# Issue order in a two-layer decoder kernel: the sums and the cast of the next weight tile ahead of the deferred work, its residues behind it

## The chip, the cores and the metric

One NeuronCore of one Trainium2 chip runs the whole program. The metric is the device time of one execution in microseconds, as the median over runs. Engines are named as in the profile: PE (TensorE, matrix products; PEld is its loading of weights), DVE (VectorE), ACT (ScalarE), POOL (GpSimd) and SP (SyncE, which issues the loads of weights).

## What is computed

A decoder trunk of two layers on 256 tokens of width 2048, in float32. Layer 0 mixes by dilated sliding-window attention, layer 1 by multi-head latent attention. Behind each mixer stands a SwiGLU of hidden width 5632, and the change touches only how these two SwiGLUs (the FFNs) are issued. Cut to what matters here:

```python
D_MODEL, SEQ, DEPTH, FFN_HIDDEN = 2048, 256, 2, 5632

def swiglu(xn, w_gu, w_down):
    g, u = jnp.split(xn @ w_gu, 2, axis=-1)
    return (jax.nn.silu(g) * u) @ w_down

for layer in range(DEPTH):
    ...                                        # layer 0: dilated attention, layer 1: latent attention
    h = h + swiglu(rms_norm(h, ffn_norm_g[layer]), ffn_w_gu[layer], ffn_w_down[layer])
return rms_norm(h, final_norm_g)
```

## The kernel before

**Products in three terms.** A float32 operand is split into a high part `hi` (a cast to the type fp32r, by ACT) and a residue `lo = raw - hi` (a subtraction on DVE). A product is then three matmuls, hi by hi, hi by lo and lo by hi, accumulated in PSUM; in `mul` these are L694, L695 and L696. Activations are kept split and transposed (`xT`, `hT`: the high halves, then the low halves).

**The stream of weights.** `WeightStream` holds all weight tiles of the program in the order in which they are used. `load` issues the DMA of a tile (1 MB, on SP's queue) into one of three `raw` slots; `split` makes `hi` and `lo` of it, in three slots each (`ahead + 1`). `next()` is called once per tile: it advances, splits up to two tiles beyond the current one, loads up to three beyond the last one split, and returns the parts of the current tile. So while the products of tile k are issued, the tile two further on is the last that has been split.

**Seven products for eight.** In the FFN the tiles come as pairs of 128-row blocks by two times 512 columns. In an "eight" pair the four blocks are multiplied with two token halves in 24 matmuls. In a "seven" pair (`kp` 2, 4 and 6 of the eight pairs of a block, except in the first block of a layer) sums of blocks replace one of the eight products: 21 matmuls. Its weight tile needs three additions on DVE beforehand (L182 to L184), and the sums get parts of their own, `th` (ACT) and `tl` (DVE). The operand's side needs sums as well (`sums`, L662 to L669, which writes `forms` or `forms_h`).

**Blocks.** `ffn` runs three parts of 16, 16 and 12 column tiles. In a part, each `j` (4 tiles) is one call of `mixed` for gate and up, eight pairs; then two calls for the down projection (`c` = 0 and 2, parts 0 and 1 alone); part 2's down projection goes through `product`. `mixed` accumulates the left half (`la`, gate) and the right half (`ra`, up) and calls `close(0, la)` in the middle of the last pair and `close(1, ra)` at its end. `close(0, ...)` returns the SiLU (L756) as a function that is issued behind the split of a tile (`ws.more()`), and `close(1, ...)` multiplies (L760).

**Deferred work.** `Later` holds functions that become due some tiles later; `later.tick()`, once per pair, issues those that are due. In the FFN these are:
- `turned`, due behind pair 0 of the next block: transposes `up` by PE (L406), splits it into `hT` (ACT L381, DVE L382), and calls `sums` for the pairs of the down projection that are "seven" (j = 4, 8 and 12 of parts 0 and 1);
- in the first block of a layer, behind pair 0, the last chunk of `transposed` with a gain (ACT L384, DVE L385) and `across` (DVE L435, PE L438, DVE L439), which lays a scale `R` out along the rows;
- `scaled(kp)`, behind pairs 2 to 7 of the first block and pairs 0 and 1 of the second: multiplies `xT` by `R` in place (L675), and calls `sums` for "seven" pairs.

**Who sets the order.** Inside the FFN, DVE and ACT run in the order in which the program issues (`tc.manual_schedule(engines=ORDERED)`). PE, POOL and SP are ordered by the framework's planner, which estimates when each instruction could start.

Of the kernel before, what the change touches and what calls it, by code (L numbers as in the profile page):

```python
# [10 lines left out]
F32 = mybir.dt.float32  # L11
F32R = mybir.dt.float32r
I32 = mybir.dt.int32
AF = mybir.ActivationFunctionType
ALU = mybir.AluOpType
AX = mybir.AxisListType

P = 128
# [70 lines left out]
class WeightStream:  # L89
# [4 lines left out]
    def __init__(self, nc, raw_pool, hl_pool, units, raw_bufs, ahead):  # L94
        self.nc, self.raw_pool, self.hl_pool, self.units = nc, raw_pool, hl_pool, units
        self.raw_bufs, self.ahead = raw_bufs, ahead
        self.raws, self.parts, self.sum_pool = {}, {}, None
        self.n_raw = self.n_split = self.at = 0

    def load(self, upto):  # L100
        while self.n_raw < min(upto, len(self.units)):
# [34 lines left out]
                    dst = [t.rearrange("p (o c) -> p o c", o=2) for t in dst]  # L136
                yield src, dst[0], dst[1], gain[:, k:k + 1]

    def split(self, upto):
        nc = self.nc  # L140
        while self.n_split < min(upto, len(self.units)):
            self.load(self.n_split + 1)
            raw = self.raws.pop(self.n_split)
            _, gain, form = self.units[self.n_split]
            if form in ("eight", "seven"):
                self.parts[self.n_split] = self.split_blocks(raw, form)
                self.n_split += 1
                continue
            _, nk, ncol = raw.shape
            if form == "dup":  # L150
                ncol *= 2
            hi = self.hl_pool.tile([P, 2048], F32R, tag="hi", name="hi", bufs=self.ahead + 1)
            lo = self.hl_pool.tile([P, 2048], F32R, tag="lo", name="lo", bufs=self.ahead + 1)
            view = lambda t: t[:, :nk * ncol].rearrange("p (k c) -> p k c", c=ncol)
            hi, lo = view(hi), view(lo)
            for src, h, l, g in self.pieces(raw, hi, lo, form, gain):
                if g is None:
                    nc.scalar.copy(out=h, in_=src)  # L158
                    nc.vector.tensor_tensor(out=l, in0=src, in1=h.bitcast(F32), op=ALU.subtract)  # L159
                else:  # L160
                    nc.scalar.activation(out=h, in_=src, func=AF.Copy, scale=g)
                    nc.vector.scalar_tensor_tensor(out=l, in0=src, scalar=g, in1=h.bitcast(F32),
                                                   op0=ALU.mult, op1=ALU.subtract)
            self.parts[self.n_split] = (hi, lo)
            self.n_split += 1

    def halve(self, hi, lo, src):
        self.nc.scalar.copy(out=hi, in_=src)  # L168
        self.nc.vector.tensor_tensor(out=lo, in0=src, in1=hi.bitcast(F32), op=ALU.subtract)  # L169

    def split_blocks(self, raw, form):

        hi, lo = [self.hl_pool.tile([P, 2048], F32R, tag=n, name=n, bufs=self.ahead + 1) for n in ("hi", "lo")]
        if form == "eight":
            self.halve(hi, lo, raw)
            return hi, lo
        th, tl = [self.sum_pool.tile([P, 1536], F32R, tag=n, name=n, bufs=1) for n in ("th", "tl")]
        sums = self.sum_pool.tile([P, 1536], F32, tag="sums", name="sums", bufs=1)  # L180
        v, w = [t.rearrange("p (i c) -> p i c", c=512) for t in (raw, sums)]
        self.nc.vector.tensor_tensor(out=v[:, 0], in0=v[:, 0], in1=v[:, 1], op=ALU.add)  # L182
        self.nc.vector.tensor_tensor(out=w[:, 1], in0=v[:, 0], in1=v[:, 2], op=ALU.subtract)
        self.nc.vector.tensor_tensor(out=w[:, 0::2], in0=v[:, 1::2],  # L184
                                     in1=w[:, 1].unsqueeze(1).broadcast_to([P, 2, 512]), op=ALU.subtract)
        self.halve(hi, lo, raw)
        self.halve(th, tl, sums)
        return hi, lo, th, tl

    def remaining(self):  # L190
        return len(self.units) - self.at
# [34 lines left out]
def kernel(ctx, tc, consts, x, attn_norm_g, ffn_norm_g, a_w_qkv, a_w_o, kv_norm_g,  # L226
                       b_w_kv_a, b_kv_a_norm_g, b_w_kv_b, b_w_q_a, b_q_a_norm_g, b_w_q_b, b_w_o,
                       ffn_w_gu, ffn_w_down, final_norm_g, out):
    nc = tc.nc
# [46 lines left out]
    rest = [ffn_norm_g.rearrange("l d -> (l d)"), kv_norm_g, b_kv_a_norm_g, b_q_a_norm_g[0]]  # L276
# [31 lines left out]
    for quad in range(HEADS // 4):  # L308
        for g in range(NG):
            k = 0  # L310
# [46 lines left out]
    later = Later()  # L357
# [283 lines left out]
    def ffn(xT, rstd, finish):  # L641

        with tc.tile_pool(name="ffn", bufs=1) as fp, tc.manual_schedule(engines=ORDERED):
# [35 lines left out]
            def mixed(X, pairs, seven, sums_of, left, right, close):  # L679

                la, ra = acc_tile(), acc_tile()
                pb, begun = None, set()

                def first(m):
                    new = m not in begun
                    begun.add(m)
                    return new  # L690

                def mul(out, x, w, i, st, sp):
                    (xh, xl), (wh, wl) = x, [t[:, i * 512:(i + 1) * 512] for t in w]
                    mm(out=out, lhsT=xh, rhs=wh, start=st, stop=False)  # L694
                    mm(out=out, lhsT=xh, rhs=wl, start=False, stop=False)  # L695
                    mm(out=out, lhsT=xl, rhs=wh, start=False, stop=sp)  # L696

                for kp in range(pairs):
                    ends = kp == pairs - 1
                    w = ws.next(late=ends)  # L700
                    x = lambda t, kk: [X[:, 2 * kp + kk, o + t * P:o + (t + 1) * P] for o in (0, S)]
                    if kp in seven:
                        i = seven.index(kp)
                        st, sp = i == 0, i == len(seven) - 1
                        if st:
                            pb = [bank() for _ in range(4)]
                        y = lambda j: x(1, 0) if j == 0 else [sums_of[:, i, h, j - 1, :] for h in range(2)]
                        mul(pb[0], x(0, 0), w[:2], 1, st, sp)
                        mul(la[:, 0], x(0, 1), w[:2], 3, first("la0"), False)
                        mul(pb[1], y(0), w[:2], 0, st, sp)  # L710
                        mul(ra[:, 0], y(3), w[:2], 2, first("ra0"), False)
                        mul(pb[3], y(2), w[2:], 0, st, sp)
                        mul(pb[2], y(1), w[2:], 1, st, sp)
                        mul(la[:, 1], x(1, 1), w[2:], 2, first("la1"), False)
                    else:
                        for i, (acc, m) in enumerate(((la, "la"), (ra, "ra"))):
                            for t in range(NT):
                                mul(acc[:, t], x(t, 0), w, 1 - i, first(f"{m}{t}"), False)
                                mul(acc[:, t], x(t, 1), w, 3 - i, False, ends)
                            if ends and i == 0:  # L720
                                then = close(0, la)
                                ws.more()
                                if then:
                                    then()
                    later.tick()
                    if seven and kp == seven[-1]:
                        nc.scalar.copy(out=left[:, 0], in_=pb[0])
                        nc.vector.tensor_tensor(out=left[:, 1], in0=pb[2], in1=left[:, 0], op=ALU.add)
                        nc.vector.tensor_tensor(out=left[:, 2], in0=pb[3], in1=left[:, 1], op=ALU.add)
                        nc.vector.tensor_tensor(out=right, in0=pb[1].unsqueeze(1).broadcast_to([P, NT, 512]),  # L730
                                                in1=left[:, 1:3], op=ALU.subtract)
                close(1, ra)

            def pair_tiles():
                return [fp.tile([P, n, 512], F32, tag=m, name=m) for m, n in (("gate", NT + 1), ("up", NT))]
# [1 line left out]
            for part, (k0, n) in enumerate(FFN_PARTS):  # L737
                last = part == len(FFN_PARTS) - 1
                hT = big_tile([P, 16, 2 * S], F32R, "hT")
                for j in range(0, n, 4):  # L740
# [7 lines left out]
                    def close(i, acc, first=first, both=(gate[:, 0:3:2], up), sc_=sc_):  # L748
                        d = both[i]
                        if not first:  # L750
                            nc.vector.tensor_tensor(out=d, in0=acc, in1=d, op=ALU.add)
                            acc = d

                        def silu():
                            for t in range(NT):
                                nc.scalar.activation(out=d[:, t], in_=acc[:, t], func=AF.Silu, scale=sc_[:, t:t + 1])  # L756
                        if i == 0:
                            return silu
                        for t in range(NT):
                            nc.vector.scalar_tensor_tensor(out=d[:, t], in0=acc[:, t], scalar=sc_[:, t:t + 1],  # L760
                                                           in1=both[0][:, t], op0=ALU.mult, op1=ALU.mult)
# [21 lines left out]
                def add(acc, c, t):  # L783
                    nc.vector.tensor_tensor(out=chunk(t, c), in0=acc[:, t, :], in1=chunk(t, c), op=ALU.add)
                    finish(c, t)
# [206 lines left out]
```

## Time and profile before

| what | value |
|---|---|
| median of 3 runs | 2678.03 us (2677.78 to 2679.45) |
| the profiled execution | 2679.72 us |
| its span, first to last instruction | 2677.9 us |
| PE busy | 2652.6 us, 99% of the span |
| PE loading weights | 2225.2 us, 83% |
| DVE busy | 2039.7 us, 76% |
| ACT busy | 1289.5 us, 48% |
| mean granted clock of PE | 0.998 |

A row of a timeline reads: start, duration, engine, line, operation, output <- inputs, shapes, count, and in brackets the engine's idle time just before it with what ended that. A row with a count over 1 stands for instructions in direct succession. Matmuls are pipelined: each is drawn longer than the distance to the next. The residue `lo` and the cast `hi` of FFN tiles are L169 and L168; `th`/`tl` have the same lines.

### The profile page before, as it was taken

The page shows a single profiled execution, that of the slowest core. Times are in us where ns is not written, and L with a number is a line of the kernel's source. Part 1 is how long each engine was busy: PE and PEld are TensorE (multiplying, and loading weights), DVE is VectorE, ACT ScalarE, POOL GpSimd, SP SyncE. Part 2 cuts the span into 40 slices and gives each one's busy share as a digit, 9 for nine tenths or more (in the row PEclk, how much of TensorE's full clock was granted, in tenths as well). Part 3 has the DMA queues.
Part 4 walks back from the last instruction along what each step waited for, and adds up shares of the span by engine and source line. Part 5 has one row for each costly group of instructions (what it writes and reads, how often), then busy time and mean ns, then how long its engine had stood idle before and what let it go on. Part 6 is the DMA issues. An engine that isn't in the chain of part 4 may idle for free. (4 is left out here: it accounts for less than half of the span.)

```text
span 2677.9 us, 32417 instructions
## 1 busy us (share of the span) xinstructions
PE 2652.6 (99%) x12914; PEld 2225.2 (83%) x12914; DVE 2039.7 (76%) x2458; ACT 1289.5 (48%) x1425; POOL 24.9 (1%) x28
## 2 busy tenths in 40 slices
PE   9999999999999999999999999999999999999998
PEld 7888888888888887788888888888887888888887
DVE  5676577477477659998899896588569988998985
ACT  5444444434444444554554454565445554544553
POOL 0000000000000000000000000000000000000000
PEclk9999999999999999999999999999999999999999
DMA  7545545555555555567567666544555676657663
GB/s 261 191 160 170 192 159 172 189 173 170 173 180 168 192 187 179 182 209 231 189 195 217 217 197 203 161 140 147 175 173 177 200 220 208 203 174 234 215 210 138
DMA packets 308088, 504.17 MB, mean 188 GB/s; under 512 B 13960, under 2 KB 117088, under 8 KB 307552
## 3 DMA queue, kind: packets, MB, share of 16 engines
q1 hardware_dynamic: 302960, 492.64, 55.8%
q0 software_dynamic: 4352, 8.39, 2.0%
q8 instruction: 101, 1.65, 0.2%
q10 hardware_dynamic: 624, 1.07, 0.1%
q14 instruction: 51, 0.42, 0.0%
HBM read 491.57 MB, written 2.10 MB: 184 GB/s over the span
## 5 line engine op out<-in xcount | busy, mean ns | idle before, releaser
L159 DVE TENSOR_TENSOR lo<-raw,hi 128x1024 fp32r<-128x1024 f32 (+2 forms) x450 | 514.7, 1167 | 338.9 <-ACT hi L158 322.7
L158 ACT CAST hi<-raw 128x1024 fp32r<-128x1024 f32 (+2 forms) x450 | 431.5, 1007 | 515.6 <-PE acc L451 291.1
L168 ACT CAST hi<-raw 128x2048 fp32r<-128x2048 f32 x240 | 458.7, 1912 | 430.9 <-issue 219.4
L169 DVE TENSOR_TENSOR lo<-raw,hi 128x2048 fp32r<-128x2048 f32 x240 | 549.4, 2290 | 76.5 <-ACT hi L168 67.8
L695 PE MATMUL acc<-lo,xT_f 128*128 128x512 f32 x988 | 387.4, 392 | 5.5 <-DVE lo L169 5.5
L694 PE MATMUL acc<-hi,xT_f 128*128 128x512 f32 x988 | 385.5, 392 | 2.7 <-ACT gate L756 2.7
L696 PE MATMUL acc<-hi,xT_f 128*128 128x512 f32 x988 | 385.4, 390 | 0.0
L451 PE MATMUL acc<-xT_a,hi 128*128 128x512 f32 x1536 | 379.4, 396 | 0.0
L451 PEld LDWEIGHTS acc<-xT_a,hi 128*128 128x128 f32 x1536 | 281.8, 189 | 53.5
L695 PEld LDWEIGHTS acc<-lo,xT_f 128*128 128x128 f32 x988 | 185.6, 188 | 48.1 <-DVE lo L169 9.9
L694 PEld LDWEIGHTS acc<-hi,xT_f 128*128 128x128 f32 x988 | 185.6, 188 | 42.9 <-ACT gate L756 3.6
L696 PEld LDWEIGHTS acc<-hi,xT_f 128*128 128x128 f32 x988 | 185.6, 188 | 39.0
L454 PEld LDWEIGHTS acc<-xT_a,lo 128*128 128x128 f32 x1536 | 196.9, 191 | 7.7
L454 PE MATMUL acc<-xT_a,lo 128*128 128x256 f32 x1536 | 199.3, 283 | 0.0
L169 DVE TENSOR_TENSOR tl<-sums,th 128x1536 fp32r<-128x1536 f32 x84 | 147.3, 1754 | 28.8 <-ACT th L168 28.8
L471 PE MATMUL acc<-lo,xT_a 128*128 128x512 f32 x384 | 150.4, 392 | 0.8 <-DVE lo L159 0.8
L472 PE MATMUL acc<-hi,xT_a 128*128 128x512 f32 x384 | 151.2, 394 | 0.0
L470 PE MATMUL acc<-hi,xT_a 128*128 128x512 f32 x384 | 151.0, 393 | 0.0
L168 ACT CAST th<-sums 128x1536 fp32r<-128x1536 f32 x84 | 124.7, 1485 | 52.6 <-PE acc L696 31.5
L695 PE MATMUL acc<-lo,hT 128*128 128x512 f32 x344 | 134.8, 392 | 2.4 <-DVE lo L169 2.4
L696 PE MATMUL acc<-hi,hT 128*128 128x512 f32 x344 | 134.1, 390 | 0.0
L694 PE MATMUL acc<-hi,hT 128*128 128x512 f32 x344 | 134.1, 392 | 0.0
(260 smaller groups left out, 4014.6 us busy)
## 6 DMA issues: line engine op xcount, KB each, us to landing
raw<-in_ffn_w_gu_dram SPq DMA_DIRECT2D x352, 512.0 KB, 4.5
raw<-in_a_w_qkv_dram SPq DMA_DIRECT2D x143, 1024.0 KB, 4.8
raw<-in_ffn_w_down_dram SPq DMA_DIRECT2D x128, 512.0 KB, 4.7
raw<-in_ffn_w_down_dram SPq DMA_DIRECT2D x24, 1024.0 KB, 5.1
raw<-in_a_w_o_dram SPq DMA_DIRECT2D x16, 1024.0 KB, 5.0
raw<-in_b_w_o_dram SPq DMA_DIRECT2D x16, 1024.0 KB, 5.1
raw<-in_b_w_kv_b_dram SPq DMA_DIRECT2D x8, 1024.0 KB, 5.2
raw<-in_b_w_q_b_dram SPq DMA_DIRECT2D x8, 768.0 KB, 4.5
```

Source lines behind the costliest of these rows:

```text
L158: nc.scalar.copy(out=h, in_=src)
L159: nc.vector.tensor_tensor(out=l, in0=src, in1=h.bitcast(F32), op=ALU.subtract)
L168: self.nc.scalar.copy(out=hi, in_=src)
L169: self.nc.vector.tensor_tensor(out=lo, in0=src, in1=hi.bitcast(F32), op=ALU.subtract)
L451: mm(out=acc[:, i, :], lhsT=sl(hi, kk), rhs=xT[:, k0 + kk, :], start=first and kk == 0, stop=False)
L454: mm(out=acc[:, i, 0:S], lhsT=sl(lo, kk), rhs=xT[:, k0 + kk, 0:S], start=False, stop=last and kk == nk - 1)
L470: mm(out=acc[:, t, :ncol], lhsT=xh, rhs=rhs(hi, kk), start=st, stop=False)
L471: mm(out=acc[:, t, :ncol], lhsT=xh, rhs=rhs(lo, kk), start=False, stop=False)
L472: mm(out=acc[:, t, :ncol], lhsT=xl, rhs=rhs(hi, kk), start=False, stop=sp)
L694: mm(out=out, lhsT=xh, rhs=wh, start=st, stop=False)
L695: mm(out=out, lhsT=xh, rhs=wl, start=False, stop=False)
L696: mm(out=out, lhsT=xl, rhs=wh, start=False, stop=sp)
```

## The change

`split` is divided in two. `steps` makes a list of a tile's instructions, each marked early or not: early are the three additions of a "seven" tile and the cast `hi`; not early are `lo`, `th` and `tl`. The new `begin` issues the early ones of the next tile to be split, and `split` later issues the rest. `mixed` calls `begin` behind every pair's products, ahead of `later.tick()`; the rest comes with the next call of `ws.next()` or `ws.more()`, behind the tick, where the whole split stood. In the same place the end of `mixed` is reordered: `close(1, ra)` and the recombination of the seven-product sums (L727 to L731) now come ahead of `begin` and of the tick. Only `mixed` calls `begin`. The order inside a tile's split is the same, and no instruction is added or removed.

```diff
@@ class WeightStream
+        self.begun = None
...
+    def halve(self, hi, lo, src, g=None, early=(True, False)):
...
+            cast = lambda: nc.scalar.copy(out=hi, in_=src)
+            rest = lambda: nc.vector.tensor_tensor(out=lo, in0=src, in1=hi.bitcast(F32), op=ALU.subtract)
...
+        return [(early[0], cast), (early[1], rest)]
...
+    def steps(self, raw, gain, form):
...
+        if form == "eight":
+            return (hi, lo), self.halve(hi, lo, raw)
+        if form == "seven":
...
+            def add():
+                tt(out=v[:, 0], in0=v[:, 0], in1=v[:, 1], op=ALU.add)
+                tt(out=w[:, 1], in0=v[:, 0], in1=v[:, 2], op=ALU.subtract)
+                tt(out=w[:, 0::2], in0=v[:, 1::2], in1=w[:, 1].unsqueeze(1).broadcast_to([P, 2, 512]),
+                   op=ALU.subtract)
+            todo = [(True, add)] + self.halve(hi, lo, raw) + self.halve(th, tl, sums, early=(False, False))
+            return (hi, lo, th, tl), todo
...
+    def begin(self):
+
+        if self.n_split < len(self.units) and self.begun is None:
+            self.load(self.n_split + 1)
+            _, gain, form = self.units[self.n_split]
+            tiles, todo = self.steps(self.raws.pop(self.n_split), gain, form)
+            for early, fn in todo:
+                if early:
+                    fn()
+            self.begun = tiles, [fn for early, fn in todo if not early]
+
+    def split(self, upto):
+        while self.n_split < min(upto, len(self.units)):
+            if self.begun is None:
...
+            else:
+                (tiles, todo), self.begun = self.begun, None
+            for fn in todo:
+                fn()
+            self.parts[self.n_split] = tiles
+            self.n_split += 1
@@ mixed, behind the products of a pair
-                    later.tick()
+                    if ends:
+                        close(1, ra)
                     if seven and kp == seven[-1]:
                         nc.scalar.copy(out=left[:, 0], in_=pb[0])
                         nc.vector.tensor_tensor(out=left[:, 1], in0=pb[2], in1=left[:, 0], op=ALU.add)
                         nc.vector.tensor_tensor(out=left[:, 2], in0=pb[3], in1=left[:, 1], op=ALU.add)
                         nc.vector.tensor_tensor(out=right, in0=pb[1].unsqueeze(1).broadcast_to([P, NT, 512]),
                                                 in1=left[:, 1:3], op=ALU.subtract)
-                close(1, ra)
+                    ws.begin()
+                    later.tick()
```

More of the change, by code (lines that the diff above doesn't have):

```diff
@@ L137, in pieces @@
                 yield src, dst[0], dst[1], gain[:, k:k + 1]
-    def split(self, upto):
+    def halve(self, hi, lo, src, g=None, early=(True, False)):
         nc = self.nc
[L141 to L171, printed above, removed]
+        if g is None:
+            cast = lambda: nc.scalar.copy(out=hi, in_=src)
+            rest = lambda: nc.vector.tensor_tensor(out=lo, in0=src, in1=hi.bitcast(F32), op=ALU.subtract)
+        else:
+            cast = lambda: nc.scalar.activation(out=hi, in_=src, func=AF.Copy, scale=g)
+            rest = lambda: nc.vector.scalar_tensor_tensor(out=lo, in0=src, scalar=g, in1=hi.bitcast(F32),
+                                                          op0=ALU.mult, op1=ALU.subtract)
@@ L175, in split_blocks @@
+        return [(early[0], cast), (early[1], rest)]
+    def steps(self, raw, gain, form):
         hi, lo = [self.hl_pool.tile([P, 2048], F32R, tag=n, name=n, bufs=self.ahead + 1) for n in ("hi", "lo")]
         if form == "eight":
[L177 to L188, printed above, removed]
+            return (hi, lo), self.halve(hi, lo, raw)
@@ new lines, in steps @@
+        if form == "seven":
+            th, tl = [self.sum_pool.tile([P, 1536], F32R, tag=n, name=n, bufs=1) for n in ("th", "tl")]
+            sums = self.sum_pool.tile([P, 1536], F32, tag="sums", name="sums", bufs=1)
+            v, w = [t.rearrange("p (i c) -> p i c", c=512) for t in (raw, sums)]
+            tt = self.nc.vector.tensor_tensor
+            def add():
[5 more added lines that the diff above has]
+            return (hi, lo, th, tl), todo
@@ new lines, in steps @@
+        _, nk, ncol = raw.shape
+        if form == "dup":
+            ncol *= 2
+        hi, lo = [t[:, :nk * ncol].rearrange("p (k c) -> p k c", c=ncol) for t in (hi, lo)]
+        return (hi, lo), [x for src, h, l, g in self.pieces(raw, hi, lo, form, gain) for x in self.halve(h, l, src, g)]
+    def begin(self):
[7 more added lines that the diff above has]
+            self.begun = tiles, [fn for early, fn in todo if not early]
@@ new lines, in split @@
+    def split(self, upto):
+        while self.n_split < min(upto, len(self.units)):
+            if self.begun is None:
+                self.load(self.n_split + 1)
+                _, gain, form = self.units[self.n_split]
+                tiles, todo = self.steps(self.raws.pop(self.n_split), gain, form)
+                todo = [fn for _, fn in todo]
+            else:
+                (tiles, todo), self.begun = self.begun, None
[3 more added lines that the diff above has]
+            self.n_split += 1
```

## The prediction

> **What bounds the kernel.** I read the page first (span, busy shares, slices), then the waits of TensorE (PE), then the timelines of VectorE (DVE), ScalarE (ACT) and PE around single waits.
>
> ```profile
> span 2677.9 us, 32417 instructions
> ...
> PE 2652.6 (99%) x12914; PEld 2225.2 (83%) x12914; DVE 2039.7 (76%) x2458; ACT 1289.5 (48%) x1425; POOL 24.9 (1%) x28
> ...
> DVE  5676577477477659998899896588569988998985
> ```
>
> PE is busy for all but 25 us, so only PE's idle time can be won. DVE's slices of 9 are the feed-forward (FFN) parts. The waits of PE, then two rows from the waits of all engines:
>
> ```profile
> PE acc L695 <- DVE lo L169: 7.9, 13, 1.0
> PE acc L694 <- ACT gate L756: 2.7, 2, 1.4
> ```
>
> ```profile
> DVE lo L169 <- ACT hi L168: 67.8, 42, 3.3
> PEld acc L695 <- DVE lo L169: 14.0, 14, 1.4
> ```
>
> Columns: total us, times, longest. PE waits 13 times for the residue `lo` of a weight tile, and twice for the SiLU that frees an accumulator. DVE in its turn waits 67.8 us for casts `hi`. One of the 13 on PE:
>
> ```profile
> 1115.63 0.39 PE L694 MATMUL acc<-hi,xT_f 128*128 128x512 f32 x1
> 1115.86 0.39 PE L695 MATMUL acc<-lo,xT_f 128*128 128x512 f32 x1
> ...
> 1127.48 0.62 PE L694 MATMUL acc<-hi,xT_f 128*128 128x512 f32 x2
> 1128.61 0.51 PE L695 MATMUL acc<-lo,xT_f 128*128 128x512 f32 x1 [0.51 <-DVE lo L169]
> 1128.95 0.40 PE L696 MATMUL acc<-hi,xT_f 128*128 128x512 f32 x1
> ```
>
> Products start 0.23 us apart but each is drawn 0.39 long. The second L694 starts at 1127.71, so L695 was due at 1127.94 and came 0.67 late: the printed idle 0.51 plus 0.16. The next start is 0.34 behind it, 0.11 too many. The 13 waits so cost 7.9 + 13 x (0.16 + 0.11) = 11.4 us, the two SiLU waits 2.7 + 2 x 0.27 = 3.2 us: 14.6 us at stake in `mixed`. What held that `lo`, on DVE:
>
> ```profile
> 1119.27 1.75 DVE L169 TENSOR_TENSOR tl<-sums,th 128x1536 fp32r<-128x1536 f32 x1
> 1120.93 1.28 DVE L382 TENSOR_TENSOR hT<-bank,hT 128x512 fp32r<-128x512 f32 x2
> 1122.13 0.68 DVE L662 TENSOR_TENSOR f<-hT 128x512 f32<-128x512 f32 x1
> ...
> 1124.45 0.56 DVE L382 TENSOR_TENSOR forms_h<-g,forms_h 128x384 fp32r<-128x384 f32 x1 [0.38 <-ACT forms_h L381]
> 1126.27 2.29 DVE L169 TENSOR_TENSOR lo<-raw,hi 128x2048 fp32r<-128x2048 f32 x1 [1.25 <-ACT hi L168]
> ```
>
> and on ACT:
>
> ```profile
> 1117.05 1.49 ACT L168 CAST th<-sums 128x1536 fp32r<-128x1536 f32 x1
> 1118.44 1.07 ACT L381 CAST hT<-bank 128x512 fp32r<-128x512 f32 x2
> 1123.23 0.30 ACT L381 CAST hT<-g 128x128 fp32r<-128x128 f32 x1 [3.72 <-DVE g L667]
> 1123.91 0.51 ACT L381 CAST forms_h<-g 128x384 fp32r<-128x384 f32 x1 [0.38 <-DVE g L667]
> 1124.33 1.91 ACT L168 CAST hi<-raw 128x2048 fp32r<-128x2048 f32 x1
> ```
>
> The reader is to see the order: behind pair 0 of a block, `later.tick()` runs `turned` (the casts and residues of `hT`, then `sums`), and only then comes the split of tile 3. ACT idles 3.72 us while its `hi` stands behind `forms_h`, and DVE then idles 1.25 us for it.
>
> **The change, part by part.** No instruction is added or removed; only places in the DVE and ACT queues change, and only where something stands between the old place and the new: pairs whose tick has work, and the last pairs, where `close(1, ra)` changes places with the tick.
>
> *(a) The cast of tile 3 ahead of `turned`.* It needs the slot of tile 0, free when pair 0 is done; pair 1 begins at about 1116.3 (three starts of 0.23 from 1115.63), while `th` holds ACT until 1118.54 anyway. So `hi` runs 1118.45 to 1120.4 and the two `hT` casts 1120.3 to 1121.4 instead of 1118.44 to 1119.5. DVE is busy with `tl` until 1121.02, and its first `hT` residue then finds its cast done; the second waits for 1121.4: 0.1 us at most. Behind `forms_h` DVE finds `hi` ready, and `lo` starts 1.25 - 0.1 = 1.15 us earlier, ending at 1127.4, before L695 is due even in plain order (1127.71). That wait goes wholly. `sums` follows in twelve blocks (three in each of parts 0 and 1, times two layers, go into the next block's pair 0 with j = 4, 8 or 12), which is twelve of the waits; the others of the 13 or 14 belong to the block behind the first.
>
> *(b) The cast ahead of the SiLU.* In the first block of a layer, at its end:
>
> ```profile
> 1018.08 0.30 ACT L381 CAST xT_f<-g 128x128 fp32r<-128x128 f32 x1 [4.55 <-DVE g L667]
> 1018.81 0.51 ACT L381 CAST forms<-g 128x384 fp32r<-128x384 f32 x1 [0.43 <-DVE g L667]
> 1019.23 1.91 ACT L168 CAST hi<-raw 128x2048 fp32r<-128x2048 f32 x1
> 1021.15 1.28 ACT L756 ACT_TABLE_LOAD   x1
> 1022.45 1.26 ACT L756 ACTIVATE gate<-acc,rstd 128x512 f32<-128x512 f32 x2
> ```
>
> ```profile
> 1022.02 0.39 PE L696 MATMUL acc<-hi,xT_f 128*128 128x512 f32 x1
> 1023.76 0.50 PE L694 MATMUL acc<-hi,xT_f 128*128 128x512 f32 x1 [1.35 <-ACT gate L756]
> ```
>
> The 1.91 us cast now goes behind pair 6's products, in the 4.55 us hole before 1018.08. It needs pair 6 done: pair 7 is 24 products of 0.23 ending at 1022.25, so from about 1016.9 to 1018.8. The casts of `sums` slip by 0.75, to about 1019.6; table load and SiLU end at 1022.3 instead of 1023.71, about when PE is free (1022.25). Gained: 3.2 less 2 x 0.1 = 3.0 us. DVE's `lo` there also starts about 0.9 us earlier.
>
> *(c) `close(1, ra)` and the recombination ahead of the tick; sums (L182 to L184) ahead of `scaled`.* DVE's total is the same. Elsewhere ticks are empty at those places: zero; uncovered, one 1.22 us `scaled` per layer would trade places with the sums, both DVE, for the same end.
>
> *(d) Left over.* In the second block of a layer DVE gains less than PE:
>
> ```profile
> 1038.86 2.29 DVE L169 TENSOR_TENSOR lo<-raw,hi 128x2048 fp32r<-128x2048 f32 x1 [1.00 <-ACT hi L168]
> ...
> 1044.98 2.29 DVE L169 TENSOR_TENSOR lo<-raw,hi 128x2048 fp32r<-128x2048 f32 x1
> ```
>
> PE arrives 1.5 earlier by (b) and some 0.4 by its own wait there; DVE some 1.0 by (b) and 1.00 by (a). That is even, but the second row's tile is used before its residue's end today only because `hi` products are put first. I leave 0.4 us there and 0.1 in the block after, times two: 1.0 us late next.
>
> *(e) The one place where the cast is in the way.* Behind pair 0 of the first block the tick holds four activations of `transposed`, then `across`, on which PE waits:
>
> ```profile
> 982.17 0.39 PE L696 MATMUL acc<-hi,xT_f 128*128 128x512 f32 x1
> ...
> 986.70 0.39 PE L694 MATMUL acc<-hi,xT_f 128*128 128x512 f32 x1
> 987.23 0.70 PE L438 MATMUL bank<-R,ones 128*128 128x256 f32 x2
> ```
>
> ```profile
> 983.03 0.47 ACT L384 ACTIVATE xT_f<-bank,g_rest 128x256 fp32r<-128x256 f32 x1 [2.73 <-PE bank L406]
> ...
> 986.17 1.90 ACT L168 CAST hi<-raw 128x2048 fp32r<-128x2048 f32 x1
> ```
>
> The cast now waits for pair 0's last product (982.17 + 0.39) and ends at 984.45; the activations start there, 1.42 us later than at 983.03, and `R` with them. If L438 keeps its place among the products, PE stands 1.42 us more per layer: 2.8 us. If the planner, which orders PE by its own estimates, moves it six products back, nothing. Today PE waits 0.3 us there (987.23 against a due 986.93), so the plan was near the truth; I take 0, with ends +2.8 and -0.6 (those two waits gone). The Trainium skill, Perfetto Trace Analysis, section Per-engine timelines, says ACT and DVE are strict FIFO. By that rule alone the sum would carry the whole 2.8 us of delay; this trace agrees as far as ACT's 3.72 us of idleness in front of a ready cast goes.
>
> *(f) Queues.* `begin` calls `load`, but the last `more()` has already loaded three tiles beyond `n_split`, so SP's order of DMAs stays; slots of `raw` come free about 1 us sooner where `lo` does. POOL's two accumulating DMAs of a down block are issued after `mixed` returns, as before.
>
> **Sum.** 11.4 - 1.0 + 3.0 - 0 = 13.4 us. The profiled execution took 2679.72 us (span 2677.9), so it would take 2666.3; against the median 2678.03, which lies 1.7 below it, 2664.6.
>
> **Rivals.**
> - *ACT's queue delays `R`* (e): 2664.6 + 2.8 = 2667.4 us. For it: the order is written out by hand there. Against: PE's order is planned. Chance 0.14.
> - *The plan of PE eats half.* PE's products are placed by estimated readiness; at 1127.48 the plan put L695 third, and it was still 0.67 late. If it now expects residues too early, half of 11.4 stays: 2664.6 + 5.7 = 2670.3. Against: a residue earlier by 1.15 ends before even the earliest place. Chance 0.14.
> - *The hole only moves.* If `hT`'s casts came so late that DVE idles 1.25 us there, `lo` stays where it is and only (b) is won: 2675.0, no change to speak of. It decides from `hi` ending at 1121.7; I have 1120.4. Chance 0.08.
> - *Slower: the slot.* If the cast, one tick earlier, found its slot taken until pair 1 ends (24 x 0.23 = 5.5 us on, about 1122.4 with the transposes), the `hT` casts behind it would end at 1125.4, 4.0 us later than in (a). `lo` would end 4.0 - 1.15 = 2.8 us later than now, in twelve blocks: 34 us, some 2712. It loses from a hold of 1.15 us on. Against: three slots, two of them with tiles still to be used, and the third freed by pair 0. Chance 0.05.
>
> **How the numbers follow.** The forecast keeps 0.59. The low end is everything won, 11.4 + 3.2 + 0.6 = 15.2, or 2662.8, less 0.8 for the spread of the runs: 2662. The high end takes in the first two rivals: 2672, which leaves out 0.13. A change under 0.2% (5.4 us) can't be told from none here. Faster: 0.59 + 0.14 + 0.14 = 0.87; same 0.08; slower 0.05.
>
> **What would show it.** In the profile after: PE L695 behind DVE `lo` down from 7.9 to 1 or 2 us; L694 behind `gate` gone; DVE `lo` behind ACT `hi` down by some 12 x 1.25 = 15 us or more; on ACT, a `hi` cast between `th` and the two `hT` casts; L438 no later behind its `R` than 0.3 us. It is wrong if the residue of tile 3 ends no earlier against its pair, or if PE shows new waits at L406, L438 or the partial banks.

## The result, and the profile after

| | before | after |
|---|---|---|
| median of the runs | 2678.38 us (4 runs) | 2664.36 us (4 runs, 2662.74 to 2664.69) |
| ratio, 95% interval | | 0.9946, 0.9929 to 0.9963 |
| the profiled execution, its span | 2679.72, 2677.9 us | 2664.17, 2662.4 us |

14.0 us went, against 13.4 forecast; the interval is 10 to 19 us. In the page of the changed kernel the busy times hardly move, PE's less than its idle time (4.8 us against 10.7):

```profile
span 2662.4 us, 32447 instructions
...
PE 2647.8 (99%) x12914; PEld 2224.4 (84%) x12914; DVE 2038.3 (77%) x2458; ACT 1289.2 (48%) x1425; POOL 24.9 (1%) x28
```

The instructions of the five engines are as many as before; the 30 that the first line has more than the page before lie outside their counts.

All waits of PE over the printing threshold in the changed kernel (columns: total us, times, longest). The line numbers are others than before: products L707 to L709, `hi` L144, `lo` L145 (of all tiles now), SiLU L771, `hT` L394 and L395, sums L166 to L168.

```profile
PE bank L419 <- DMA xt<-in_x_dram: 2.3, 1, 2.3
PE bank L268 <- DVE mhalf L388: 1.1, 1, 1.1
PE acc L464 <- ACT vb L921: 0.7, 1, 0.7
PE acc L464 <- DVE ccT L398: 0.5, 1, 0.5
PE bank L419 <- ACT cc L865: 0.4, 1, 0.4
PE acc L483 <- DVE qn L503: 0.2, 1, 0.2
```

The rows for `lo` (7.9 us) and `gate` (2.7 us) are gone, and so is the one for `R`. The wait for `xt` is that for the input at the start of the program; it was 1.1 us before and 0.7 to 2.7 in the experiments, 1.5 in the first, which has the change left out. DVE's waits for `hi` of all tiles fell from 390.5 (322.7 + 67.8) to 374.6 us, by the 15 or so that were forecast. The same block as in the prediction, in the timeline of DVE and then of ACT after:

```profile
1115.81 1.75 DVE L145 TENSOR_TENSOR tl<-sums,th 128x1536 fp32r<-128x1536 f32 x1
1117.48 1.28 DVE L395 TENSOR_TENSOR hT<-bank,hT 128x512 fp32r<-128x512 f32 x2
...
1120.99 0.56 DVE L395 TENSOR_TENSOR forms_h<-g,forms_h 128x384 fp32r<-128x384 f32 x1 [0.38 <-ACT forms_h L394]
1121.47 2.28 DVE L145 TENSOR_TENSOR lo<-raw,hi 128x2048 fp32r<-128x2048 f32 x1
```

```profile
1113.59 1.49 ACT L144 CAST th<-sums 128x1536 fp32r<-128x1536 f32 x1
1114.98 1.90 ACT L144 CAST hi<-raw 128x2048 fp32r<-128x2048 f32 x1
1116.79 1.06 ACT L394 CAST hT<-bank 128x512 fp32r<-128x512 f32 x2
1119.78 0.30 ACT L394 CAST hT<-g 128x128 fp32r<-128x128 f32 x1 [1.93 <-DVE g L680]
```

The cast stands between `th` and `hT`, ACT's idle hole is 1.93 us instead of 3.72, and `lo` follows `forms_h` with no idle time. From the start of `tl` to that of `lo` it takes 5.66 us, where it took 7.00. PE takes the residue in its plain place:

```profile
1124.02 0.40 PE L707 MATMUL acc<-hi,xT_f 128*128 128x512 f32 x1
1124.25 0.39 PE L708 MATMUL acc<-lo,xT_f 128*128 128x512 f32 x1
1124.48 0.39 PE L709 MATMUL acc<-hi,xT_f 128*128 128x512 f32 x1
```

`lo` ends at 1123.75, 0.5 us ahead of L708, and 0.27 ahead of the load of its weights, which PEld does at 1124.02. This slack is the number on which the experiments turn.

### The profile page after: what moved, and what is told of

The parts are those of the page before. It is cut to its first block, busy times and chain, and to the rows that moved or that the text cites. A ratio compares the mean times of both kernels' runs of the same rounds, so it can differ in the third digit from the quotient of the medians.

```text
span 2662.4 us, 32447 instructions
## 1 busy us (share of the span) xinstructions
PE 2647.8 (99%) x12914; PEld 2224.4 (84%) x12914; DVE 2038.3 (77%) x2458; ACT 1289.2 (48%) x1425; POOL 24.9 (1%) x28
## 5 line engine op out<-in xcount | busy, mean ns | idle before, releaser
L145 DVE TENSOR_TENSOR lo<-raw,hi 128x1024 fp32r<-128x1024 f32 (+3 forms) x690 | 1063.6, 1557 | 398.0 <-ACT hi L144 374.6
L144 ACT CAST hi<-raw 128x1024 fp32r<-128x1024 f32 (+3 forms) x690 | 890.5, 1321 | 975.7 <-PE acc L464 300.4
L707 PE MATMUL acc<-hi,xT_f 128*128 128x512 f32 x988 | 387.3, 392 | 0.0
L708 PE MATMUL acc<-lo,xT_f 128*128 128x512 f32 x988 | 385.9, 391 | 0.0
L709 PE MATMUL acc<-hi,xT_f 128*128 128x512 f32 x988 | 384.9, 390 | 0.0
L707 PEld LDWEIGHTS acc<-hi,xT_f 128*128 128x128 f32 x988 | 185.5, 188 | 40.3 <-ACT gate L771 0.8
L709 PEld LDWEIGHTS acc<-hi,xT_f 128*128 128x128 f32 x988 | 185.5, 188 | 39.7
L708 PEld LDWEIGHTS acc<-lo,xT_f 128*128 128x128 f32 x988 | 185.5, 188 | 38.6
L145 DVE TENSOR_TENSOR tl<-sums,th 128x1536 fp32r<-128x1536 f32 x84 | 147.3, 1753 | 29.1 <-ACT th L144 29.1
L144 ACT CAST th<-sums 128x1536 fp32r<-128x1536 f32 x84 | 124.6, 1483 | 53.6 <-PE acc L709 31.8
L707 PE MATMUL acc<-hi,hT 128*128 128x512 f32 x344 | 134.6, 391 | 0.0
L708 PE MATMUL acc<-lo,hT 128*128 128x512 f32 x344 | 134.3, 390 | 0.0
L709 PE MATMUL acc<-hi,hT 128*128 128x512 f32 x344 | 134.0, 389 | 0.0
L168 DVE TENSOR_TENSOR sums<-raw,sums 128x1024 f32<-128x1024 f32 x84 | 102.9, 1225 | 2.9
L484 PEld LDWEIGHTS acc<-lo,xT_a 128*128 128x128 f32 x384 | 72.4, 188 | 15.6 <-DVE lo L145 1.0
```

What stands on the lines that cost most here:

```text
L144: cast = lambda: nc.scalar.copy(out=hi, in_=src)
L145: rest = lambda: nc.vector.tensor_tensor(out=lo, in0=src, in1=hi.bitcast(F32), op=ALU.subtract)
L168: tt(out=w[:, 0::2], in0=v[:, 1::2], in1=w[:, 1].unsqueeze(1).broadcast_to([P, 2, 512]), op=ALU.subtract)
L484: mm(out=acc[:, t, :ncol], lhsT=xh, rhs=rhs(lo, kk), start=False, stop=False)
```

## Experiments

The theory: the place of the cast `hi` in ACT's queue is the whole gain, behind pair 0 for the residue waits and behind pair 6 of the first block for the SiLU. The rivals: the rearranged DVE work, the sums ahead of the tick, or PE's planned order. Ratios are to runs of the kernel before on the same chip. Edits are shown against the changed kernel, cut to the lines that matter.

**1. The reordering alone.** `begin` is not called, so each split stands whole behind the tick:

```diff
-                    ws.begin()
                     later.tick()
```

> Only the reordering of close(1, ra) and of the recombination (L727 to L731) ahead of the tick; begin is not called, so each tile's split stands whole behind the tick as before. Theory (the place of the cast hi is everything): no change, 2678.4 us within 1 us, PE still waits 7.9 us for lo and 2.7 us for gate. Rival (the order of DVE's own work at the end of a block is what helps): part of the 14 us, so 2671 us or less.

Measured: 2679.42 us against 2679.11, ratio 1.0001 (0.9992 to 1.001). Its waits of PE are those of before to the tenth:

```profile
PE acc L708 <- DVE lo L145: 7.9, 13, 1.0
PE acc L707 <- ACT gate L770: 2.7, 2, 1.4
```

So `close(1, ra)` and the recombination ahead of the tick bring nothing.

**2. The early part behind pair 0 alone**, in all blocks but the first of a layer; the end of `mixed` as before:

```diff
-                    if ends:
-                        close(1, ra)
+                    if kp == 0 and not unscaled:
+                        ws.begin()
+                    later.tick()
...
-                    ws.begin()
-                    later.tick()
+                close(1, ra)
```

`unscaled`, a new argument of `mixed`, is true in the first block of a layer.

> begin is called behind pair 0 alone, in every block but the first of a layer; close(1, ra) and the recombination stand as before. Theory: this is term (a), 11.4 us: all waits of PE for lo (7.9 us, 13) go, 2667.0 us; the two waits for gate (2.7 us) stay. Rival (PE's planned order gives half back): 2672 to 2673 us, with waits of PE for lo of 3 us and more.

Measured: 2667.58 us, ratio 0.9956 (0.9944 to 0.9969), 11.5 us less than before. Term (a) was 11.4. The row for `lo` in the FFN is gone, the one for `gate` is unchanged:

```profile
PE acc L707 <- ACT gate L771: 2.7, 2, 1.4
```

So PE's planned order gave nothing back.

**3. The early part behind pair 6 of the first block alone.** As in experiment 2, but with

```diff
+                    if kp == 6 and unscaled:
+                        ws.begin()
+                    later.tick()
```

> begin is called behind pair 6 of the first block of a layer alone; the rest as before. Theory: term (b), the two waits for gate (2.7 us) all but go, 3.0 us; but PE then comes 1.5 us earlier to tile 3 of the second block and DVE only 0.9, so that wait for lo grows by 0.6 us in each layer: 3.0 - 1.2 = 1.8 us net, 2676.6 us, waits for lo up from 7.9 to about 9 us. Rival (the terms simply add): 2675.4 us.

Measured: 2676.86 us, ratio 0.9991 (0.9982 to 1.0): 2.3 us less, between the two, and the interval doesn't part them. The trace does:

```profile
PE acc L708 <- DVE lo L145: 8.5, 14, 1.0
```

The `gate` row is gone, and the waits for `lo` rose from 7.9 to 8.5 with one wait more: part of what PE won at the SiLU it met again at the residue of the second block, as expected but with 0.6 us of idle time instead of 1.1. Experiments 2 and 3 together give 11.5 + 2.3 = 13.8 of the 14.0 us.

**4. The whole split ahead of the tick**, residues too, in the same places:

```diff
             for early, fn in todo:
-                if early:
-                    fn()
-            self.begun = tiles, [fn for early, fn in todo if not early]
+                fn()
+            self.begun = tiles, []
```

> begin issues the whole split (also lo, th and tl) ahead of the tick, in the places of the change. Theory: nothing is left to win, since PE waits for no residue any more: 2664.4 us within 1 us; the residue of tile 3 ends some 3 to 4 us ahead of its pair instead of 0.5, and R of the first block comes about 2 us later still, which the planned order of PE takes up. Rival (work of the tick pushed back on DVE makes a new wait): 2667 us or more, with new waits of PE at L451, L419 or the partial banks.

Measured: 2688.56 us, ratio 1.0035 (1.0021 to 1.0049): slower than before, 24 us slower than the change. Of the two expectations the rival was right that it loses, but neither had the place. The line numbers are one lower here. No residue is late any more, but:

```profile
PE acc L706 <- ACT gate L770: 10.0, 2, 5.0
```

The waits of all engines hold a second row, of PE's weight loads:

```profile
PEld acc L706 <- issue: 12.6, 26, 0.5
```

DVE and PE around one of those 26:

```profile
1111.74 2.28 DVE L145 TENSOR_TENSOR lo<-raw,hi 128x2048 fp32r<-128x2048 f32 x1
1113.93 1.22 DVE L765 TENSOR_TENSOR gate<-acc,gate 128x1024 f32<-128x1024 f32 x1
```

```profile
1114.82 0.39 PE L708 MATMUL acc<-hi,xT_f 128*128 128x512 f32 x1
1115.30 0.47 PE L706 MATMUL acc<-hi,xT_f 128*128 128x512 f32 x1
1115.60 0.40 PE L707 MATMUL acc<-lo,xT_f 128*128 128x512 f32 x1
```

Behind pair 6, the residue of the tile begun there now stands on DVE ahead of `close(0, la)` (L765), which frees the accumulator that the next block needs first. L765 ends at 1115.15, and PE's next block starts 0.48 us behind its last product instead of 0.23, with 0.07 more behind it: 26 x 0.32 = 8.3 us. In the first block of a layer the same residue and those before it put off the `sums` of pair 4 on DVE, behind those stand the casts of the sums on ACT, and behind them the SiLU: 5.0 us, twice. That is 18.3 of 24; some 3 us more are told at the end, and some 2 us stay open.

**5. The same, but behind pair 6 only the early part.**

```diff
-                if early:
+                if early or whole:
                     fn()
...
-                    ws.begin()
+                    ws.begin(kp != pairs - 2)
```

> As the run with the whole split ahead of the tick, but behind pair 6 (where the next thing on DVE and ACT is close(0, la) and the SiLU) begin issues only the early part, as the change does. Theory: the 24 us lost there came from lo, 2.29 us on DVE, standing ahead of close(0, la) (0.25 us per block, and 5 us in each first block, where the sums' casts and the SiLU queue up behind it on ACT); with the residue back behind close(0, la) it is all regained: 2664.4 us within 1.5 us, no wait of PE for gate over 0.3 us. Rival (residues ahead of turned and scaled cost as well): 2668 us or more.

Measured: 2671.11 us, ratio 0.9971 (0.9961 to 0.9982), 7 us short of the expectation. The 26 waits went, but not those for `gate`:

```profile
PE acc L707 <- ACT gate L771: 5.6, 2, 2.8
```

Residues ahead of `scaled` behind the earlier pairs of the first block were enough to put off the `sums`, and the SiLU behind their casts. On DVE there:

```profile
1015.21 2.29 DVE L145 TENSOR_TENSOR lo<-raw,hi 128x2048 fp32r<-128x2048 f32 x1 [1.25 <-ACT hi L144]
1017.42 2.35 DVE L688 TENSOR_TENSOR xT_f<-xT_f,R 128x1024 fp32r<-128x1024 f32 x2
1019.81 0.69 DVE L675 TENSOR_TENSOR f<-xT_f 128x512 f32<-128x512 f32 x1
```

The `sums` (L675) start at 1019.81, in the changed kernel at 1016.54, and both FFNs begin at the same time (976.73 and 976.74).

**6. The same, and in the first block only the early part throughout.** Against experiment 5:

```diff
-                    ws.begin(kp != pairs - 2)
+                    ws.begin(kp != pairs - 2 and not unscaled)
```

> As the run with the whole split ahead of the tick except behind pair 6, but in the first block of a layer begin issues only the early part, as the change does. Theory: what was still lost (6.9 us against the change) came from the first block alone, where lo ahead of scaled put off the sums of pair 4 on DVE, the SiLU behind their casts on ACT, and PE by 2.8 us (and 1.6 us more at half clock) per layer; without it 2664.4 us within 1.5 us, no wait of PE for gate over 0.3 us, and the residue of tile 3 some 4.5 us ahead instead of 0.5: more slack and no time. Rival (residues ahead of turned cost in the other blocks too): 2667 us or more.

Measured: 2662.99 us, ratio 0.9942 (0.9928 to 0.9955), not to be told from the change's 0.9946. The order on DVE in the same block:

```profile
1115.00 1.75 DVE L145 TENSOR_TENSOR tl<-sums,th 128x1536 fp32r<-128x1536 f32 x1
1116.67 2.28 DVE L145 TENSOR_TENSOR lo<-raw,hi 128x2048 fp32r<-128x2048 f32 x1
1118.87 1.28 DVE L395 TENSOR_TENSOR hT<-bank,hT 128x512 fp32r<-128x512 f32 x2
```

`lo` is through before `hT`'s residues begin, some 4.5 us ahead of its pair. So residues ahead of `turned` cost nothing and win nothing; what was lost in 4 and 5 lay at `close(0, la)` and in the first block.

**7 and 8. A hold behind the cast.** Copies on ACT that nothing reads, between the begun cast and the tick, behind pair 0 of every block but the first of a layer; five copies (`range(5)`), then one (`range(1)`):

```diff
                     ws.begin()
+                    if kp == 0 and not unscaled:
+                        for _ in range(5):
+                            nc.scalar.copy(out=held.rearrange("p (a b) -> p a b", b=P), in_=ident.unsqueeze(1).broadcast_to([P, 3, P]))
                     later.tick()
```

> The change, with five extra copies of 384 columns on ACT (some 0.43 us each, 2.1 us) between the cast that begin issues behind pair 0 and the tick, in every block but the first of a layer: a cast that holds up hT's casts for longer, as the rival of the occupied slot has it. Theory: hT's residues start 2.0 us later on DVE, lo of tile 3 ends 2.0 us later against 0.5 us of slack, so PE waits some 1.5 us (1.2 us if hi products are put first) in each of the twelve blocks with sums: 2664.4 + 14 to 19, 2678 to 2683 us, so nothing is left of the gain. Rival (the planned order of PE or DVE's slack takes it up): under 2670 us.

Measured with five: 2688.1 us, ratio 1.0038 (1.0024 to 1.0052), slower than before. ACT, and the waits of PE, where L709 is now the product with `lo`:

```profile
1116.99 2.70 ACT L750 COPY held<-ident 128x384 f32<-128x384 f32 x5
1119.60 1.07 ACT L394 CAST hT<-bank 128x512 fp32r<-128x512 f32 x2
```

```profile
PE acc L709 <- DVE lo L145: 20.7, 12, 2.0
```

The hold was 2.61 us (1116.99 to 1119.60), 0.52 a copy instead of the 0.43 reckoned. Less the slack of 0.5 that leaves 2.1 late; the twelve waits cost 20.7 + 12 x (0.16 + 0.11) = 23.9 us, 2.0 each, and the kernel is 23.8 us slower than with one copy. They are the twelve blocks with `sums`.

> The same with one extra copy (0.43 us): a hold below the slack of 0.5 us. Theory: no more than 0.1 us per block is lost, 2664.4 us within 1.5 us. Rival (every delay of hT's casts goes on to PE): 12 x 0.43 = 5 us, 2669.5 us.

Measured with one: 2664.34 us, ratio 0.9948 (0.9935 to 0.996): no loss that can be told from none. The hold was 0.41 us (1117.95 to 1118.36), and `lo` ended 0.14 us ahead of its product. The products came in time, but the loads of the weights ahead of them already waited:

```profile
PEld acc L709 <- DVE lo L145: 2.5, 12, 0.6
```

So 0.41 us of hold is about all that is hidden, and 2.61 us cost 2.0 in each of twelve blocks, which puts the line at some 0.6 us (an estimate from these two runs). Below the slack nothing, above it the loss twelve times: as far as two holds can show it, that is how the prediction drew the line between residue and pair. The Trainium skill, Perfetto Trace Analysis, section Per-engine timelines, has ACT and DVE as strict FIFO. The trace of five copies agrees for ACT: casts of `hT` whose inputs were there waited 2.61 us behind copies that nobody reads.

**9. Without the sums.** `begin` passes over "seven" tiles:

```diff
-        if self.n_split < len(self.units) and self.begun is None:
+        if self.n_split < len(self.units) and self.begun is None and self.units[self.n_split][2] != "seven":
```

> The change, but begin leaves seven tiles alone, so that their additions L182 to L184 and their casts stand behind the tick as before. Theory: the sums ahead of the tick bring nothing, since where a seven tile is begun the tick is empty or holds a single scaled on DVE: 2664.4 us within 1 us. Rival (the sums are part of the gain): 2666 us or more, with waits of PE for lo in the second block of a layer.

Measured: 2663.73 us, ratio 0.9946 (0.9934 to 0.9959). The gain is that of the casts of "eight" tiles; what the additions ahead of the tick bring is too small for the medians to show.

**The FFNs alone.** Runs of one kernel differ by up to 4 us, more than most of these terms. In the traces most of it arises ahead of the FFNs: the first one begins anywhere from 974.65 to 977.95 us. The time from the first to the last product that reads `xT_f` (all of an FFN but the down projection of its last part) leaves this out. One execution of each kernel, in us:

| kernel | FFN of layer 0 | of layer 1 | both, less than before |
|---|---|---|---|
| before | 646.42 | 646.46 | |
| changed | 638.86 | 638.84 | 15.18 |
| 1, order only | 646.44 | 646.44 | 0.00 |
| 2, pair 0 only | 640.62 | 640.65 | 11.61 |
| 3, pair 6 only | 645.43 | 645.35 | 2.10 |
| 4, whole split | 650.49 | 650.46 | -8.07 |
| 5, whole but pair 6 | 643.10 | 643.24 | 6.54 |
| 6, whole but first block | 638.82 | 638.81 | 15.25 |
| 7, five copies | 650.92 | 650.71 | -8.75 |
| 8, one copy | 639.22 | 638.82 | 14.84 |
| 9, without sums | 639.05 | 639.05 | 14.78 |

The layers agree within 0.4 us. The change won 15.2 us in the FFNs, one copy costs 0.3 us of that, and the early part of the "seven" tiles is worth 0.4. In experiment 5 the loss against the change is 8.6 us by this count; the medians had 6.7.

## Why the prediction was right

**(a) 11.4 us** was 11.5 by the medians of experiment 2 and 11.6 by its FFNs. `lo` came 1.34 us earlier against `tl` (7.00 to 5.66) instead of 1.15: `hT`'s residues lost nothing by the later casts, and back to back with `forms_h` the next instruction starts before the other's drawn end.

**(b) 3.0 us.** ACT at the end of the first block, and PE there:

```profile
1016.57 1.91 ACT L144 CAST hi<-raw 128x2048 fp32r<-128x2048 f32 x1 [3.52 <-PE acc L709]
...
1019.29 1.28 ACT L771 ACT_TABLE_LOAD   x1 [0.20 <-PE acc L709]
1020.59 1.27 ACT L771 ACTIVATE gate<-acc,rstd 128x512 f32<-128x512 f32 x2
```

```profile
1021.54 0.39 PE L709 MATMUL acc<-hi,xT_f 128*128 128x512 f32 x1
1021.91 0.50 PE L707 MATMUL acc<-hi,xT_f 128*128 128x512 f32 x1
1022.25 0.40 PE L708 MATMUL acc<-lo,xT_f 128*128 128x512 f32 x1
```

The cast starts as pair 6 ends and the SiLU ends 0.05 us ahead of the next block's first product. PE loses 0.14 there and 0.11 behind it, where 0.1 was left: 2 x 0.25 instead of 3.2, or 2.7 won. The cast is out of the SiLU's way altogether: ACT now waits 0.20 us for PE's own product ahead of the table load. Alone (experiment 3) the change in this place is worth 2.1 by the FFNs, since PE then meets the residue.

**(c) 0** is confirmed by experiment 1 for the reordering (0.0 in the FFNs). For the sums it is 0.4 us won, by the FFNs of experiment 9.

**(d) 1.0 us left over** was the term mis-sized: it is 0. No wait for `lo` remains in the FFN. PE's order still has three `hi` products first in pair 4 of the second block, at 1044.16, and DVE gained more than reckoned: the `lo` of that tile starts at 1042.15 instead of 1044.98, 2.6 us earlier within the FFN, where 2.0 were reckoned.

**(e) 0, with ends +2.8 and -0.6.** The delay on ACT came as computed: the first activation starts at 984.24, 1.21 us later than before, or 1.42 with the 0.21 us by which this execution's FFN started sooner.

```profile
984.24 0.47 ACT L397 ACTIVATE xT_f<-bank,g_rest 128x256 fp32r<-128x256 f32 x1
```

```profile
987.62 0.39 PE L709 MATMUL acc<-hi,xT_f 128*128 128x512 f32 x1
987.85 0.39 PE L707 MATMUL acc<-hi,xT_f 128*128 128x512 f32 x1
988.12 0.70 PE L451 MATMUL bank<-R,ones 128*128 128x256 f32 x2
```

PE's order put L451 six products further back, and its wait for `R` is gone: the low end, some 0.6 us won.

The terms as measured, 11.6 + 2.7 + 0.4 + 0.6, make 15.3, and the FFNs shrank by 15.2: that is about the sum which the prediction had at its low end, everything won. The mechanism held term by term; that 13.4 came so near to the 14.0 of the medians is in part luck, since (d) and (e) were set too low by 1.6 us together and the medians, with the spread of the program's start in them, have 1.2 less than the FFNs. Of the rivals, the delayed `R` was shut out by the rows just above, the plan of PE by experiment 2, the moved hole by the timeline of DVE. The rival of the occupied slot did not occur, but experiment 7 made its hold and got its kind of loss; its point of loss against the kernel before, a hold of 1.15 us, was not tested: the holds were 0.41 and 2.61 us.

## What to carry to other kernels

Where two in-order engines hand work to each other, look for the engine that idles in front of an instruction that could already run, and move that instruction alone up to where its inputs are ready; its consumer may stay. Moving more of the same chain is not more of the same: the residues, moved along, won nothing where they were harmless and cost 24 us where they stood ahead of the work on which the next block's accumulator waits. Reckon each wait against its slack, because a delay below it is free, and one above it is paid in every block that has the wait.

## What was not expected

A wait of PE can cost again behind its end. In experiment 5 PE stood idle for 2.79 us in each layer; in layer 0 the products behind that:

```profile
1024.74 0.79 PE L707 MATMUL acc<-hi,xT_f 128*128 128x512 f32 x1 [2.79 <-ACT gate L771]
1025.33 0.63 PE L708 MATMUL acc<-lo,xT_f 128*128 128x512 f32 x1
1025.76 0.63 PE L709 MATMUL acc<-hi,xT_f 128*128 128x512 f32 x1
```

They start 0.43 us apart instead of 0.23. One stretch of each of two kernels (its length in us, then busy times of PE, PEld, DVE, ACT and POOL, then the granted clock, the share of the DMA engines and their GB/s): the first is of experiment 5 behind that wait, the second of the kernel before, behind its wait of 1.35 us at the same place:

```profile
1024.70:1028.10 3.40, 3.36 (x8) 2.68 (x9) 3.33 (x6) 1.13 (x1) 0.00 (x0) 0.53 0.60 166
```

```profile
1023.70:1027.10 3.40, 3.33 (x15) 2.77 (x16) 3.36 (x5) 0.44 (x2) 0.00 (x0) 1.00 0.75 225
```

The clock was 0.53 for about 3.4 us. Eight starts, from 1024.74 to 1028.13, took 3.39 us where 1.8 are usual: 1.6 us on top of the wait, and much the same in layer 1. In experiment 4, behind 5.0 us, it was alike, 3 us of what is missing there.

The length of the idle time alone does not decide it. Behind 1.35 us, and behind 1.70 us in experiment 7, the clock stayed at 1.00. But at the start of the program, where PE waits for the input, it was 0.59 from 10.4 to 13.8 us in the kernel before, behind waits of 1.13 and 0.65 us, and 1.00 in experiment 1, behind 1.46 and 0.65 us. What decides between the two no run here shows; it is part of the spread of the start that the table of the FFNs leaves out. The Trainium skill, TensorE: Matmul & The Clock Gate, Part 1, puts the half clock behind an idle window of about 3.4 us; here 2.79 us of idle time was followed by it in both layers, so the measurement decides.
